# A scan over 64-token chunks: products taken from the array's two row halves in turn, and recurrent states read without block-diagonal copies

## The chip, the core and the metric

The kernel runs on one core of one Trainium2 chip, in float32 throughout. The metric is the device time of one execution in microseconds (us). The other seven cores do nothing.

## The reference, cut to what matters

One layer of a hybrid backbone over 128 context tokens and 1024 latent tokens, 1024 channels: a SwiGLU, a token mixer, a second SwiGLU, each followed by a layer norm. The change touches the recurrent branch of the mixer alone, a scan in two directions over 16 heads of 64 channels:

```python
def _rwkv7_step(S, inp):
    r, w, k, v, kk, a = inp
    sa = jnp.einsum('dbhvk,dbhk->dbhv', S, kk)
    S = S * w[..., None, :] - sa[..., :, None] * (kk * a)[..., None, :] + v[..., :, None] * k[..., None, :]
    return S, jnp.einsum('dbhvk,dbhk->dbhv', S, r)
...
s_final, y = lax.scan(_rwkv7_step, s0.astype(f32), xs)
```

Context tokens start from zero states, latent tokens from cached states. The final context states are an output.

## The kernel before, in words

The program has four stages: the first SwiGLU, the mixer's input projections and preparation, the scan, and at the end the output projections with the second SwiGLU. The change lies in the scan stage (the `with pool("s1")` block).

The 1152 tokens are cut into 18 chunks of 64 tokens, and the 16 heads into two halves of 8. So there are 36 steps. Each step treats one chunk of the forward direction (d = 0) and one of the backward direction (d = 1) for 8 heads. A tile holds two heads on its 128 partitions: the even head (e = 0) on partitions 0 to 63, the odd head (e = 1) on 64 to 127, and four such pairs i. A step consists of these pieces, all float32 on TensorE:

- `pre_lm` (line 987, tile `pa`): for each direction, pair and e, a product with a contraction over one head's 64 channels, so over one row half of the array, 128 by 128 out. VectorE multiplies it by a mask into `LM` (line 988). It is done a step or two ahead. The calls `pre_lm(s, d, 0)` and `pre_lm(s, d, 1)` are separate, with 4 products each.
- `pre_kb` (line 994, tile `pt`): transposes, copied to `KBT` by ScalarE (line 996).
- `main(s)`: line 1015 multiplies by the states. Its moving operand is `Sb`, a 128x128 tile per pair with the even head's 64x64 state in one corner and the odd head's in the other, so one product over all 128 rows serves two heads. Line 1020 adds `LM` times the values in the same accumulator `xy` (one tile of one PSUM bank per direction). ScalarE copies the sum to `Xs` (line 1024). Line 1028 multiplies by the inverse `W`, back into `xy`. ScalarE writes its negative to `vu` (line 1032). Line 1038 makes the state update `sp`. VectorE adds it to the state `Sc` (line 1039), GpSimd multiplies `Sc` by the chunk's decay (line 1040), and ScalarE copies both corners to `Sb` (lines 1041 and 1042). Line 1046 completes the outputs in `xy`, and ScalarE copies them to `yt` (line 1049).

In lines 1020, 1028 and 1046 the loop over the heads takes the two directions in turn. Their operands lie on opposite partition halves, and so do their results.

Between these pieces `fill` issues products of other work (lines 852, 854, 856: gate projections of the mixer, 128x384, in a format of one pass). They are dealt out by a table (`SPREAD`), the same number per step. A float32 product stands in the trace as two matmul records, here called passes; a transpose and a filler product are one.

Every four steps VectorE also gets one `solve`: the inversion of 32x32 triangular blocks, a chain of 31 pairs of a multiply and a subtract (lines 744 and 746) with some transposes (755 and 758). It starts from a tile `Gq`, of which one half comes by DMA into `Gt` and through ScalarE (line 739). Its result is needed some steps later.

The order of the instructions on each engine is set by a scheduler when the program is built. It runs its own timeline, so the order in the queues is not the order of the source, and each engine then takes its queue strictly as written.

Of the kernel before, what the change touches and what calls it, by code (L numbers as in the profile page):

```python
# [8 lines left out]
F32 = mybir.dt.float32  # L9
F32R = mybir.dt.float32r  # L10
AF = mybir.ActivationFunctionType
ALU = mybir.AluOpType
# [4 lines left out]
P = 128  # L17
# [43 lines left out]
def tile_step(ctx: ExitStack, tc: tile.TileContext, I: dict, O: dict):  # L61
    nc = tc.nc
    V, A, G, S, PE = nc.vector, nc.scalar, nc.gpsimd, nc.sync, nc.tensor
# [378 lines left out]
    PCst = cpool.tile([P, 2, NCHUNK, NP], F32, name="PCst")  # L442
# [10 lines left out]
    with pool("facc") as facc, pool("f1w", side="right") as wmore, pool("f1p", 6, psum=True) as psum, pool("f1a", 2, psum=True) as paux:  # L453
# [6 lines left out]
        with pool("st") as sp:  # L460
# [458 lines left out]
        for n in (6, 7):  # L919
            yield from back(*prev, n)  # L920

    with pool("s1") as pl, pool("spa", 2, psum=True) as psA, pool("spx", 2, psum=True) as psX, \
            pool("spg", 2, psum=True) as psG, pool("spm", 2, psum=True) as psM:
        maskLM = [sc[:, 0:128], sc[:, 128:256]]
        TAGP[0] = "m"
        states = {}
        for q in range(2):
            for d in range(2):
                states[q, d] = (pl.tile([P, 4, 64], F32, name=f"Sc{q}{d}"), states[0, d][1] if q else pl.tile([P, 4, P], F32, name=f"Sb{d}"))
# [4 lines left out]

        def init_ctx(hb):
            for d in range(2):
                Sc, Sb = states[0, d]
                G.memset(Sc, 0.0)
                G.memset(Sb, 0.0)
                S.dma_start(states[1, d][0], I["state"][d][:, 4 * hb:4 * hb + 4])  # L940

        def init_lat():
            for d in range(2):
                Sc, Sb = states[1, d]
                A.copy(Sb[0:64, :, 0:64], Sc[0:64])
                A.copy(Sb[64:128, :, 64:128], Sc[64:128])

        ctxs = {}

# [25 lines left out]
                c["ak"][s].append(ak)  # L975
            c["LM"][s], c["KBT"][s] = {}, {}

        def pre_lm(s, d, e):
            c = ctxs[s // 2]
            ak = c["ak"][s][d]  # L980
            if e == 0:
                c["LM"][s][d] = pl.tile([P, 4, 2, P], F32, name=f"LM{d}", tag=f"LM{d}", bufs=2)
            mk = maskLM[d].unsqueeze(1).broadcast_to([P, 4, P])
            es = slice(e * 64, e * 64 + 64)
            pa = psA.tile([P, 4, P], F32, name="pa", tag="pa")
            for i in range(4):
                PE.matmul(pa[:, i, :], ak[es, i, 128:256], ak[es, i, 0:128], start=True, stop=True)  # L987
            V.tensor_tensor(c["LM"][s][d][:, :, e, :], pa, mk, ALU.mult)

        def pre_kb(s, d):  # L990
            c = ctxs[s // 2]
# [6 lines left out]
        def main(s):  # L998
# [13 lines left out]
            for d in range(2):  # L1012
                Sb = states[q, d][1]
                for i in range(4):
                    PE.matmul(xys[d][:, 2 * i:2 * i + 2, :], ak[d][:, i, 0:128], Sb[:, i, :], start=(i == 0), stop=False, skip_group_check=True)  # L1015
            for h in range(8):
                for d in range(2):
                    x0, x1 = XR[d]
                    y0, y1 = YR[d]
                    last = PE.matmul(xys[d][x0:x1, h, :], LM[d][y0:y1, h // 2, h % 2, x0:x1], vu[d][y0:y1, h, :], start=False, stop=True, skip_group_check=True)  # L1020
            between(s, 0, last)
            for d in range(2):
                x0, x1 = XR[d]
                A.copy(Xs[x0:x1], xys[d][x0:x1])
            for h in range(8):
                for d in range(2):
                    x0, x1 = XR[d]
                    last = PE.matmul(xys[d][x0:x1, h, :], W[d][x0:x1, h // 2, h % 2, :], Xs[x0:x1, h, :], start=True, stop=True, skip_group_check=True)
            between(s, 1, last)
            for d in range(2):  # L1030
                x0, x1 = XR[d]
                A.mul(vu[d][x0:x1], xys[d][x0:x1], -1.0)
            for d in range(2):
                Sc, Sb = states[q, d]
                sp = psM.tile([P, 4, 64], F32, name="sp", tag="m")
                for h in range(8):
                    e = slice((h % 2) * 64, (h % 2) * 64 + 64)
                    PE.matmul(sp[e, h // 2, :], KBT[d][:, h // 2, e], vu[d][:, h, :], start=True, stop=True)
                V.tensor_tensor(Sc, Sc, sp, ALU.add)
                G.tensor_tensor(Sc, Sc, PCst[:, d, cs[d], 4 * hb:4 * hb + 4].unsqueeze(2).broadcast_to([P, 4, 64]), ALU.mult)  # L1040
                A.copy(Sb[0:64, :, 0:64], Sc[0:64])
                A.copy(Sb[64:128, :, 64:128], Sc[64:128])
            for h in range(8):
                for d in range(2):
                    y0, y1 = YR[d]
                    last = PE.matmul(xys[d][y0:y1, h, :], LM[d][:, h // 2, h % 2, y0:y1], vu[d][:, h, :], start=False, stop=True, skip_group_check=True)  # L1046
            for d in range(2):
                y0, y1 = YR[d]
                A.copy(yt[y0:y1, m[d]], xys[d][y0:y1])
# [59 lines left out]
        pre(1)  # L1109
        for s in range(2):  # L1110
            for d in range(2 - s):
                pre_lm(s, d, 0)
                pre_lm(s, d, 1)
                pre_kb(s, d)
        fl = filler(psG)
        sols = [(2, solve(1, psM))]
# [27 lines left out]
        with ExitStack():  # L1144
            for s in range(n):
                if s == 18:
                    init_ctx(1)
                if s % 18 == 2:
                    init_lat()
# [12 lines left out]
                if s + 2 < n:  # L1162
# [8 lines left out]
                hb, j = s // 18, s % 18  # L1171
                if j == 1:
                    for d in range(2):
                        S.dma_start(O["st"][d][:, 4 * hb:4 * hb + 4], states[0, d][0])
# [184 lines left out]
```

## Time and profile before

| | |
|---|---|
| median of 3 runs | 3506.33 us (3505.05 to 3511.2) |
| profiled execution, first to last instruction | 3503.5 us |
| scan stage in it | 1660 to 2388 us, 728 us |
| busy in the scan stage: TensorE, VectorE, ScalarE, GpSimd | 682.8, 380.5, 375.1, 261.4 us |
| share of the DMA engines in the scan stage | 0.63 |
| mean granted TensorE clock, whole span and scan stage | 0.964 and 0.96 |

The profile gives no time for the profiled execution but its span. The median of the three runs shown is 2.8 us longer than that span. A row of instructions by group reads: line, engine, operation, tiles written and read, shapes, count, then busy time in us, mean duration of one in ns, and the engine's idle time just before them with what ended it. A row of the timeline reads: start and length in us, then the same names, and how many follow each other. The length reaches to the modelled end of the last one, so the pitch of n passes is (length minus one duration) over n - 1.

### The profile page before, as it was taken

Reading aid. Unit: us, or ns where it says so; the run is one execution under the profiler, and the core shown is the slowest. Engines: PE = TensorE matmul, PEld = TensorE weight load, DVE = VectorE, ACT = ScalarE, POOL = GpSimd, SP = SyncE. Lnnn points to the kernel's source line nnn. Section 1 sums busy time; section 2 is a strip of 40 time slices with the busy share of each in tenths; the row PEclk is TensorE's granted clock in tenths of the full one; section 3 lists DMA queues with packets and bytes.
Section 4 is the critical chain, followed back from the end, with each engine's and each line's share of the span. In section 5 each row is a group of like instructions: output and inputs, shape, how many; then the busy total and the mean of one; then the engine's idle time right before and its main releaser. Section 6 shows DMA issues by size and latency. Waiting matters only on the chain. (4 is left out here: it accounts for less than half of the span.)

```text
span 3503.5 us, 61793 instructions
## 1 busy us (share of the span) xinstructions
PE 3325.9 (95%) x25166; PEld 3150.8 (90%) x25166; DVE 1962.7 (56%) x3237; ACT 1224.6 (35%) x2107; POOL 1348.6 (38%) x1077
## 2 busy tenths in 40 slices
PE   7999999999999999799999989998999999999997
PEld 7999999999988877598888888887999999999996
DVE  6888633357556788756365656534574332222466
ACT  4111111125534444532545555555345111111133
POOL 5111211136556666653322443157774111111144
PEclk9999999999999998799999989998999999999998
DMA  6443211123544545476557667665541111111133
GB/s 230 132 141 128 90 37 49 37 97 127 205 156 151 169 149 161 142 220 191 174 165 213 205 175 224 186 183 183 200 169 49 43 37 49 41 45 40 47 127 107
DMA packets 311421, 461.57 MB, mean 132 GB/s; under 512 B 115552, under 2 KB 211296, under 8 KB 309600
## 3 DMA queue, kind: packets, MB, share of 16 engines
q1 hardware_dynamic: 311136, 457.62, 41.1%
q8 instruction: 198, 3.24, 0.4%
q14 instruction: 87, 0.71, 0.1%
HBM read 325.44 MB, written 110.69 MB: 124 GB/s over the span
## 5 line engine op out<-in xcount | busy, mean ns | idle before, releaser
L127 POOL TENSOR_TENSOR wl<-wr,wh 128x1024 fp32r<-128x1024 f32 (+1 forms) x168 | 386.3, 2300 | 716.8 <-ACT wh L125 647.9
L125 ACT CAST wh<-wr 128x1024 fp32r<-128x1024 f32 (+1 forms) x321 | 321.9, 1012 | 829.8 <-PE po L135 424.0
L271 POOL TENSOR_TENSOR gl<-sg,gh 128x384 fp32r<-128x384 f32 x132 | 159.7, 1210 | 787.1 <-ACT gh L270 787.1
L134 PE MATMUL po<-gh,wh 128*128 128x384 f32 x1056 | 357.5, 339 | 8.5 <-ACT gh L270 4.2
L135 PE MATMUL pg<-h1l,wh 128*128 128x384 f32 x1056 | 356.4, 338 | 6.8 <-POOL h1l L143 6.8
L135 PE MATMUL po<-gl,wh 128*128 128x384 f32 x1056 | 357.3, 338 | 1.7 <-POOL gl L271 1.7
L136 PE MATMUL pg<-h3h,wl 128*128 128x384 f32 x1056 | 357.9, 339 | 0.0
L134 PE MATMUL pg<-h3h,wh 128*128 128x384 f32 x1056 | 357.6, 340 | 0.0
L134 PE MATMUL pg<-h1h,wh 128*128 128x384 f32 x1056 | 357.5, 339 | 0.0
L135 PE MATMUL pg<-h3l,wh 128*128 128x384 f32 x1056 | 356.8, 338 | 0.0
L136 PE MATMUL pg<-h1h,wl 128*128 128x384 f32 x1056 | 355.5, 337 | 0.0
L136 PE MATMUL po<-gh,wl 128*128 128x384 f32 x1056 | 355.5, 337 | 0.0
L127 DVE TENSOR_TENSOR wl<-wr,wh 128x1024 fp32r<-128x1024 f32 x153 | 223.2, 1463 | 214.8 <-ACT wh L125 214.7
L134 PE MATMUL pm<-h2h,wh 128*128 128x384 f32 x936 | 327.9, 350 | 8.5 <-ACT ga L810 5.1
L268 DVE TENSOR_TENSOR sg<-sg,pg 128x384 f32<-128x384 f32 x132 | 74.1, 561 | 464.9 <-PE pg L136 454.9
L135 PE MATMUL pm<-h2l,wh 128*128 128x384 f32 x936 | 328.3, 351 | 0.0
L136 PE MATMUL pm<-h2h,wl 128*128 128x384 f32 x936 | 328.3, 351 | 0.0
L288 DVE SCALAR_TENSOR_TENSOR ac<-po,modh,ac 128x384 f32<-128x384 f32 (+1 forms) x352 | 172.6, 515 | 95.4 <-PE po L136 95.4
L379 DVE SCALAR_TENSOR_TENSOR fm<-fm 128x512 f32<-128x512 f32 x224 | 183.8, 821 | 53.3 <-DMA fm<-in_w_mod 50.2
L134 PEld LDWEIGHTS po<-gh,wh 128*128 128x128 f32 x1056 | 199.2, 189 | 11.8 <-ACT gh L270 4.8
L135 PEld LDWEIGHTS pg<-h1l,wh 128*128 128x128 f32 x1056 | 200.3, 190 | 9.5 <-POOL h1l L143 8.9
L270 ACT CAST gh<-sg 128x384 fp32r<-128x384 f32 x132 | 67.5, 512 | 394.9 <-DVE sg L268 394.8
(289 smaller groups left out, 7681.3 us busy)
## 6 DMA issues: line engine op xcount, KB each, us to landing
wr<-in_ffn_in SPq DMA_DIRECT2D x120, 512.0 KB
ak<-ak SPq DMA_DIRECT2D x48, 768.0 KB
ak<-ak SPq DMA_DIRECT2D x72, 512.0 KB
wr<-in_w_mix SPq DMA_DIRECT2D x63, 512.0 KB
wr<-in_ffn_out SPq DMA_DIRECT2D x60, 512.0 KB
fm<-in_w_mod SPq DMA_DIRECT2D x112, 256.0 KB
sh<-pads SPq DMA_DIRECT2D x108, 130.0 KB
wr<-in_w_o SPq DMA_DIRECT2D x24, 512.0 KB
```

What stands on the lines that cost most here:

```text
L125: A.copy(h[:, :w], r[:, :w])
L127: e.tensor_tensor(l[:, :w], r[:, :w], h[:, :w].bitcast(F32), ALU.subtract)
L134: PE.matmul(ps, wh, xh, start=first and k == 0, stop=False)
L135: PE.matmul(ps, wh, xl, start=False, stop=False)
L136: PE.matmul(ps, wl, xh, start=False, stop=last and k == n - 1)
L268: lastv[0] = V.tensor_tensor(sg, sg, pu[:, :BN], ALU.mult)
L270: A.copy(gs[j, b][0][:, sl], sg)
L271: G.tensor_tensor(gs[j, b][1][:, sl], sg, gs[j, b][0][:, sl].bitcast(F32), ALU.subtract)
L288: lastv[0] = V.scalar_tensor_tensor(accs[b][:, n, s0:s1], po[:, s0:s1], modh[:, gate_i // 4, n, g:g + 1], accs[b][:, n, s0:s1], ALU.mult, ...
L379: V.scalar_tensor_tensor(jk, w, 1.0, silc[:, s, hf * 512:hf * 512 + 512], ALU.mult, ALU.mult, accum_out=part[:, kt, s, hf:hf + 1])
```

## The change: what it does

1. The block-diagonal copies `Sb` are gone, with the ScalarE copies that filled them and the two initial copies. The state product (now line 1010) multiplies `Sc` as it is, one head at a time: 16 products per step over 64 rows with 64 columns, in place of 8 over 128 rows with 128 columns. The heads e = 0 and e = 1 alternate.
2. `pre_lm` makes both e at once, product by product in turn, into two `pa` tiles. It is called once per step and direction, where there were two calls.
3. `xy` becomes one tile of two PSUM banks with a single buffer. A bank now holds the heads of one e for both directions; before, a bank held all heads of one direction.
4. The product with `W` (now line 1026) goes to a tile `us` of its own, one bank for both directions, from the pool that also holds `sp`, `pt` and the solve's products.
5. For d = 1, VectorE makes the copy to `Xs` (now line 1021) and the negative to `vu` (now line 1031). ScalarE keeps d = 0. The multiplication of `Sc` by the decay moves from GpSimd to VectorE (now line 1041).

```diff
@@ the scan stage
-    ... pool("spx", 2, psum=True) as psX
+    ... pool("spx", 1, psum=True) as psX
...
-        def pre_lm(s, d, e):
+        def pre_lm(s, d):
...
-            es = slice(e * 64, e * 64 + 64)
-            pa = psA.tile([P, 4, P], F32, name="pa", tag="pa")
+            pa = [psA.tile([P, 4, P], F32, name="pa", tag="pa") for e in range(2)]
             for i in range(4):
-                PE.matmul(pa[:, i, :], ak[es, i, 128:256], ak[es, i, 0:128], start=True, stop=True)
-            V.tensor_tensor(c["LM"][s][d][:, :, e, :], pa, mk, ALU.mult)
+                for e in range(2):
+                    es = slice(e * 64, e * 64 + 64)
+                    PE.matmul(pa[e][:, i, :], ak[es, i, 128:256], ak[es, i, 0:128], start=True, stop=True)
+            for e in range(2):
+                V.tensor_tensor(LM[:, :, e, :], pa[e], mk, ALU.mult)
...
-            xys = [psX.tile([P, 8, 64], F32, name="xy", tag="xy") for d in range(2)]
-            for d in range(2):
-                Sb = states[q, d][1]
-                for i in range(4):
-                    PE.matmul(xys[d][:, 2 * i:2 * i + 2, :], ak[d][:, i, 0:128], Sb[:, i, :], start=(i == 0), stop=False, skip_group_check=True)
+            xy = psX.tile([P, 2, 2, 4, 64], F32, name="xy", tag="xy")
+            eh = lambda t: t.rearrange("p (i e) v -> p e i v", e=2)
+            for i in range(4):
+                for d in range(2):
+                    for e in range(2):
+                        es = slice(e * 64, e * 64 + 64)
+                        PE.matmul(xy[:, e, d, i, :], ak[d][es, i, 0:128], states[q, d][es, i, :], start=(i == 0 and d == 0), stop=False,
+                                  skip_group_check=True)
...
-                A.copy(Xs[x0:x1], xys[d][x0:x1])
+                (V.tensor_copy if d else A.copy)(eh(Xs[x0:x1]), xy[x0:x1, :, d])
+            us = psM.tile([P, 8, 64], F32, name="us", tag="m")
...
-                    last = PE.matmul(xys[d][x0:x1, h, :], W[d][x0:x1, h // 2, h % 2, :], Xs[x0:x1, h, :], start=True, stop=True, skip_group_check=True)
+                    last = PE.matmul(us[x0:x1, h, :], W[d][x0:x1, h // 2, h % 2, :], Xs[x0:x1, h, :], start=True, stop=True, skip_group_check=True)
...
-                A.mul(vu[d][x0:x1], xys[d][x0:x1], -1.0)
+                if d:
+                    V.tensor_scalar(vu[d][x0:x1], us[x0:x1], -1.0, None, ALU.mult)
+                else:
+                    A.mul(vu[d][x0:x1], us[x0:x1], -1.0)
...
                 V.tensor_tensor(Sc, Sc, sp, ALU.add)
-                G.tensor_tensor(Sc, Sc, PCst[:, d, cs[d], 4 * hb:4 * hb + 4].unsqueeze(2).broadcast_to([P, 4, 64]), ALU.mult)
-                A.copy(Sb[0:64, :, 0:64], Sc[0:64])
-                A.copy(Sb[64:128, :, 64:128], Sc[64:128])
+                V.tensor_tensor(Sc, Sc, PCst[:, d, cs[d], 4 * hb:4 * hb + 4].unsqueeze(2).broadcast_to([P, 4, 64]), ALU.mult)
...
-            if s + 1 < n:
-                pre_lm(s + 1, 1, k)
+            if s + 1 < n and k == 0:
+                pre_lm(s + 1, 1)
...
-                    pre_lm(s + 2, 0, 0)
+                    pre_lm(s + 2, 0)
                 fill(2)
                 sol(s)
-                if s + 2 < n:
-                    pre_lm(s + 2, 0, 1)
                 fill(3)
```

The scheduler writes the queues anew, so the change moves more than the source tells. Three places matter.

TensorE, the state product and the product with `LM` in one step. The tiles `vu0` and `LM0` belong to d = 0, `vu1` and `LM1` to d = 1. Before:

```order
L1015 MATMUL xy_17666<-Sb0_14605,ak0_17254 128x128 x4
L1020 MATMUL xy_17666<-vu0_1_13546,LM0_17258 64x64 x4
L1015 MATMUL xy_17667<-Sb1_14607,ak1_17256 128x128 x4
L1020 MATMUL xy_17667<-vu1_1_13548,LM1_17411 64x64 x4
L1020 MATMUL xy_17666<-vu0_1_13546,LM0_17258 64x64
```

Now:

```order
L1010 MATMUL xy_16693<-Sc10_14606,ak0_16295 128x64 x2
L1010 MATMUL xy_16693<-Sc11_14607,ak1_16297 128x64 x2
L1016 MATMUL xy_16693<-vu0_1_13546,LM0_16299 64x64
L1016 MATMUL xy_16693<-vu1_1_13548,LM1_16446 64x64
L1016 MATMUL xy_16693<-vu0_1_13546,LM0_16299 64x64
```

Before, the two directions had accumulators of their own, and the queue took four products of one direction and then four of the other before it took them in turn. Now the accumulator is one tile, all state products stand ahead of all products with `LM`, and these alternate by direction from the first on.

TensorE, the products of `pre_lm`. Each `pa` tile belongs to one e, so to one row half. Now, at two steps:

```order
L979 MATMUL pa_16559<-ak0_16554 128x128
L979 MATMUL pa_16560<-ak0_16554 128x128
L979 MATMUL pa_16559<-ak0_16554 128x128
```

```order
L979 MATMUL pa_16837<-ak0_16832 128x128 x3
L1026 MATMUL us_16748<-Xs_16692,W_16046 64x64
L979 MATMUL pa_16837<-ak0_16832 128x128
L1026 MATMUL us_16748<-Xs_16692,W_16046 64x64 x15
L852 MATMUL pb_16589<-u2_14777,wh_16463 128x384
```

In the first the row halves alternate as the source has them. In the second the queue takes all four products of one half, and those of the other half (`pa_16838`) only after the products with `W` and fillers. Of the 576 products, 279 stand beside one of the other half and 297 do not.

VectorE, in a step in which a solve runs. Now:

```order
L744 TENSOR_TENSOR pr<-Wd,Gq 128x23x9
L1021 COPY Xs<-xy 64x2x4x64
L746 TENSOR_TENSOR Wd<-Wd,pr 128x23x9
L981 TENSOR_TENSOR LM_15940<-pa,sc 128x4x128
L744 TENSOR_TENSOR pr<-Wd,Gq 128x24x8
```

```order
L744 TENSOR_TENSOR pr<-Wd,Gq 128x30x2
L1031 TENSOR_SCALAR vu_0_13547<-us 64x512
L746 TENSOR_TENSOR Wd<-Wd,pr 128x30x2
```

The copy to `Xs` and the negative to `vu`, for which TensorE waits in mid-step, now stand between instructions of the solve, here 14 of them from the one to the other. From one step's first state addition to the next step's, the queue before held at most 31 instructions of a solve; now the fullest interval of each of the seven solves in the loop holds 37, 39, 38, 29, 28, 35 and 42 (before: 30, 29, 29, 31, 29, 27 and 26).

After the scan the TensorE queue is the same as before.

More of the change, by code (lines that the diff above doesn't have):

```diff
@@ L920, in filler @@
             yield from back(*prev, n)
-    with pool("s1") as pl, pool("spa", 2, psum=True) as psA, pool("spx", 2, psum=True) as psX, \
+    with pool("s1") as pl, pool("spa", 2, psum=True) as psA, pool("spx", 1, psum=True) as psX, \
             pool("spg", 2, psum=True) as psG, pool("spm", 2, psum=True) as psM:
@@ L928, in tile_step @@
             for d in range(2):
-                states[q, d] = (pl.tile([P, 4, 64], F32, name=f"Sc{q}{d}"), states[0, d][1] if q else pl.tile([P, 4, P], F32, name=f"Sb{d}"))
+                states[q, d] = pl.tile([P, 4, 64], F32, name=f"Sc{q}{d}")
         base = [(0, (0, 1)), (0, (1, 0))] + [(1, (2 + i, 17 - i)) for i in range(16)]
@@ L936, in init_ctx @@
             for d in range(2):
[L937 to L942, printed above, removed]
-            for d in range(2):
-                Sc, Sb = states[1, d]
-                A.copy(Sb[0:64, :, 0:64], Sc[0:64])
-                A.copy(Sb[64:128, :, 64:128], Sc[64:128])
+                G.memset(states[0, d], 0.0)
+                S.dma_start(states[1, d], I["state"][d][:, 4 * hb:4 * hb + 4])
         ctxs = {}
@@ L976, in pre @@
             c["LM"][s], c["KBT"][s] = {}, {}
-        def pre_lm(s, d, e):
+        def pre_lm(s, d):
             c = ctxs[s // 2]
             ak = c["ak"][s][d]
-            if e == 0:
-                c["LM"][s][d] = pl.tile([P, 4, 2, P], F32, name=f"LM{d}", tag=f"LM{d}", bufs=2)
+            LM = c["LM"][s][d] = pl.tile([P, 4, 2, P], F32, name=f"LM{d}", tag=f"LM{d}", bufs=2)
             mk = maskLM[d].unsqueeze(1).broadcast_to([P, 4, P])
-            es = slice(e * 64, e * 64 + 64)
-            pa = psA.tile([P, 4, P], F32, name="pa", tag="pa")
+            pa = [psA.tile([P, 4, P], F32, name="pa", tag="pa") for e in range(2)]
             for i in range(4):
-                PE.matmul(pa[:, i, :], ak[es, i, 128:256], ak[es, i, 0:128], start=True, stop=True)
-            V.tensor_tensor(c["LM"][s][d][:, :, e, :], pa, mk, ALU.mult)
+                for e in range(2):
[3 more added lines that the diff above has]
+                V.tensor_tensor(LM[:, :, e, :], pa[e], mk, ALU.mult)
         def pre_kb(s, d):
@@ L1010, in main @@
             yt = c["yt"]
-            xys = [psX.tile([P, 8, 64], F32, name="xy", tag="xy") for d in range(2)]
-            for d in range(2):
-                Sb = states[q, d][1]
-                for i in range(4):
-                    PE.matmul(xys[d][:, 2 * i:2 * i + 2, :], ak[d][:, i, 0:128], Sb[:, i, :], start=(i == 0), stop=False, skip_group_check=True)
+            xy = psX.tile([P, 2, 2, 4, 64], F32, name="xy", tag="xy")
[6 more added lines that the diff above has]
+                                  skip_group_check=True)
             for h in range(8):
@@ L1019, in main @@
                     y0, y1 = YR[d]
-                    last = PE.matmul(xys[d][x0:x1, h, :], LM[d][y0:y1, h // 2, h % 2, x0:x1], vu[d][y0:y1, h, :], start=False, stop=True, skip_group_check=True)
+                    last = PE.matmul(xy[x0:x1, h % 2, d, h // 2, :], LM[d][y0:y1, h // 2, h % 2, x0:x1], vu[d][y0:y1, h, :], start=False, stop=True,
+                                     skip_group_check=True)
             between(s, 0, last)
@@ L1045, in main @@
                     y0, y1 = YR[d]
-                    last = PE.matmul(xys[d][y0:y1, h, :], LM[d][:, h // 2, h % 2, y0:y1], vu[d][:, h, :], start=False, stop=True, skip_group_check=True)
+                    last = PE.matmul(xy[y0:y1, h % 2, d, h // 2, :], LM[d][:, h // 2, h % 2, y0:y1], vu[d][:, h, :], start=False, stop=True,
+                                     skip_group_check=True)
             for d in range(2):
                 y0, y1 = YR[d]
-                A.copy(yt[y0:y1, m[d]], xys[d][y0:y1])
+                A.copy(eh(yt[y0:y1, m[d]]), xy[y0:y1, :, d])
                 if s % 2 == 1 and other(cs[d] // 2, d) <= s % 18:
@@ L1111, in tile_step @@
             for d in range(2 - s):
-                pre_lm(s, d, 0)
-                pre_lm(s, d, 1)
+                pre_lm(s, d)
                 pre_kb(s, d)
@@ L1147, in tile_step @@
                     init_ctx(1)
-                if s % 18 == 2:
-                    init_lat()
                 after[0] = main(s)
@@ L1173, in tile_step @@
                     for d in range(2):
-                        S.dma_start(O["st"][d][:, 4 * hb:4 * hb + 4], states[0, d][0])
+                        S.dma_start(O["st"][d][:, 4 * hb:4 * hb + 4], states[0, d])
                 for tt in range(9):
```

4 lines of the change are left out of this document (1 added, 3 removed).

## The prediction

> **What bounds the kernel now.** I read the stretches first, to see how full TensorE is in the scan stage, then its groups there, then single stretches of its timeline for the price of a pass, then the waits, then VectorE.
>
> ```profile
> 1660.00:2388.00 728.00, 682.82 (x9619) 611.29 (x9616) 380.53 (x771) 375.08 (x699) 261.39 (x230) 0.96 0.63 187
> ```
>
> The columns are stretch, length, busy time of TensorE, its weight loads, VectorE, ScalarE and GpSimd, then granted clock, DMA share and GB/s. TensorE is busy 683 of 728 us; the other 45 it waits. So TensorE work taken away is time, unless a wait takes its place. Who ends these waits:
>
> ```profile
> PE sp L1038 <- ACT vu L1032: 15.4, 7, 5.7
> PE pt L994 <- DVE Sc L1039: 14.4, 7, 3.0
> PE pa L987 <- DVE LM L988: 6.1, 5, 3.6
> PE xy L1028 <- ACT Xs L1024: 4.0, 1, 4.0
> ```
>
> VectorE ends 20.5 us of them, ScalarE 19.4. On average VectorE is half idle (380 of 728), but not where a solve runs:
>
> ```profile
> 2229.58 0.41 DVE L1039 TENSOR_TENSOR Sc<-Sc,sp 128x256 f32<-128x256 f32 x1
> 2244.70 0.41 DVE L1039 TENSOR_TENSOR Sc<-Sc,sp 128x256 f32<-128x256 f32 x1
> ...
> 2232.00:2242.00 10.00, 10.00 (x123) 8.99 (x121) 9.55 (x22) 5.38 (x11) 1.28 (x1) 1.00 0.47 151
> ```
>
> From one state addition to the next step's, 15.1 us pass here, and within them VectorE is busy 9.55 of 10 us and TensorE 10 of 10. In such a step both are full: lighten one and load the other, and the other sets the pace.
>
> **The price of a pass on TensorE.**
>
> ```profile
> 24.43 1.84 PE L481 MATMUL pmod<-cc,w 128*128 128x2 f32 x16
> 2101.02 1.02 PE L1020 MATMUL xy<-vu,LM 64*64 64x64 f32 x14
> 2105.38 1.71 PE L987 MATMUL pa<-ak 64*128 64x128 f32 x16
> 2116.74 1.50 PE L1015 MATMUL xy<-Sb,ak 128*128 128x128 f32 x12
> 2118.18 1.15 PE L1020 MATMUL xy<-vu,LM 64*64 64x64 f32 x32
> 2123.12 1.16 PE L987 MATMUL pa<-ak 64*128 64x128 f32 x8
> 2124.21 0.44 PE L854 MATMUL pb<-u,wh 128*128 128x384 f32 x1
> ```
>
> ```profile
> L987 PE MATMUL pa<-ak 64*128 64x128 f32 x1145 | 151.2, 290 | 6.1 <-DVE LM L988 6.1
> L1015 PE MATMUL xy<-Sb,ak 128*128 128x128 f32 x576 | 79.7, 282 | 0.1
> L1046 PE MATMUL xy<-vu,LM 128*64 128x64 f32 x1152 | 57.3, 238 | 0.0
> L1020 PE MATMUL xy<-vu,LM 64*64 64x64 f32 x1152 | 56.1, 223 | 0.0
> L1028 PE MATMUL xy<-Xs,W 64*64 64x64 f32 x1152 | 52.2, 226 | 4.0 <-ACT Xs L1024 4.0
> ```
>
> Pitch is (length minus one duration) by (count minus one). The state products: (1.50 - 0.28) / 11 = 0.111 us. Line 481 has weights just as wide but only 2 columns: (1.84 - 0.25) / 15 = 0.106, no cheaper. So with 128-wide weights a pass costs 0.11 us, however few its columns. Line 1020 with one direction alone: (1.02 - 0.22) / 13 = 0.061. With both in turn: (1.15 - 0.22) / 31 = 0.030. Opposite halves run side by side. Last, changing the array's shape: the 8 passes from 2123.12 to the next start at 2124.21 take 1.09 us, 0.19 more than 8 x 0.112. That is what a stretch of another shape costs.
>
> **The change part by part, TensorE.** Counts are from the queues, prices from the rows above.
>
> *State products.* Before, 16 passes per step at 0.112. Now 32, as 16 side-by-side pairs with 128-wide weights, at 0.112 a pair. Gain 0. The bounds: if 64 columns brought the price of 0.061, it is 16 x 0.05 x 36 = 29 us less; if the halves don't overlap, 16 x 0.112 x 36 = 64 us more. Line 481 decides for the middle.
>
> *`pre_lm`.* A product is two passes, 0.224 us alone, 0.112 as one of a pair. The queue lets 279 of the 576 alternate: -31 us. The other 297 gain nothing, since the scheduler put one half's four products ahead of the other's. But the old queue already had some 37 places where one half's four directly follow the other's, and there the array overlapped them: the 16 passes at 2105.38 took 1.71, where 16 x 0.112 and one entry and tail (0.1 + 0.18) make 2.07. That is 37 x 0.36 = 13 us already had. Net -18.
>
> *Products with `LM` and `W`.* Today's groups are busy 56.1 + 52.2 = 108 us. Wholly in turn they would take 36 x 1.15 x 2 = 83, or 86 at the stage's clock of 0.96. The old queue takes all 16 in turn in only 14 steps (`LM`) and 11 (`W`), the new one in 33 and 30. So about -21.
>
> *Outputs (line 1046, now 1045).* Some 110 products stood in one-direction stretches, and now next to none; each saves one of its two passes of 0.06: -6.
>
> *Shapes.* Outside the products with `LM` and `W`, whose stretches are in their busy time, the queue's stretches of one shape go from 409 to 414: +1.
>
> Sum on TensorE: 0 - 18 - 21 - 6 + 1 = **-44 us**.
>
> **VectorE.** It gets four instructions a step.
>
> ```profile
> L744 DVE TENSOR_TENSOR pr<-Wd,Gq 128x31 f32<-128x31 f32 (+15 forms) x221 | 107.4, 486 | 64.8 <-ACT vu L1032 21.8 <-PE sp L1038 20.5 <-DMA Wd<-in_id 16.4
> L988 DVE TENSOR_TENSOR LM<-pa,sc 128x512 f32<-128x512 f32 x144 | 96.4, 684 | 113.1 <-PE pa L987 103.9 <-PE xy L1046 8.7
> L746 DVE TENSOR_TENSOR Wd<-Wd,pr 128x135 f32<-128x135 f32 (+15 forms) x222 | 95.5, 430 | 5.7
> L1039 DVE TENSOR_TENSOR Sc<-Sc,sp 128x256 f32<-128x256 f32 x72 | 29.9, 417 | 70.7 <-PE sp L1038 68.2 <-ACT wh L125 2.0
> ...
> L1032 ACT ACTIVATE vu<-xy 64x512 f32<-64x512 f32 x72 | 42.6, 592 | 40.2 <-PE xy L1028 39.2
> L1024 ACT COPY Xs<-xy 64x512 f32<-64x512 f32 x72 | 41.8, 581 | 57.2 <-PE xy L1020 56.4
> L1041 ACT COPY Sb<-Sc 64x256 f32<-64x256 f32 x71 | 28.7, 405 | 61.6 <-POOL Sc L1040 60.7
> L1042 ACT COPY Sb<-Sc 64x256 f32<-64x256 f32 x71 | 28.6, 402 | 1.4
> ...
> L1040 POOL TENSOR_TENSOR Sc<-Sc,PCst 128x256 f32<-128x256 f32 x71 | 45.3, 649 | 121.3 <-DVE Sc L1039 119.1 <-PE pt L994 2.2
> ```
>
> None of the four stands on VectorE in the trace. For `Xs` and `vu` the nearest rows are ScalarE's 0.58 and 0.59, and VectorE's 0.68 for a tile of the same width from PSUM; I take 0.6 (0.55 to 0.7). For the decay the nearest is the addition of the same size, 0.42; GpSimd's 0.65 is the upper end. Together 2 x 0.6 + 2 x 0.42 = 2.0 us a step, 73 us in all. In the steps without a solve VectorE's idle half covers it.
>
> In the fullest step of a solve nothing does. An instruction of a solve is (107.4 + 95.5) / 443 = 0.46 us. Before, that step holds about 29 of them: 13.3 us, with two additions (0.8), three masks (2.0) and a gate product (0.5) 16.7 us, about TensorE's own. Now it holds 28 to 42, on average 35: 16.1 + 3.3 + 2.0 = 21.4 us. TensorE's step falls by 44 / 36 = 1.2 to about 15.5. And TensorE can't run ahead, since `Xs` and `vu` stand in mid-queue and their time within the step is fixed too. So it waits about 6 us in this step and some 1.5 in the fuller neighbour: 7.5 x 7 solves = 53 us, where VectorE ends 20.5 today: **+33**. The bounds: 20.5 again (0 more), if VectorE does the queue's solve work in the idle time of the neighbouring steps; 75 (+55), if each point at which TensorE waits in the step adds its own lateness.
>
> *The solve's start.* VectorE also stands still until `Gq` is there:
>
> ```profile
> 1811.63 1.92 ACT L739 COPY Gq<-Gt 64x1024 f32<-64x1024 f32 x1 [4.42 <-DMA Gt<-qd]
> 1814.22 1.12 PE L1038 MATMUL sp<-vu,KBT 128*64 128x64 f32 x16 [5.74 <-ACT vu L1032]
> 1814.90 0.19 DVE L744 TENSOR_TENSOR pr<-Wd,Gq 128x31 f32<-128x31 f32 x1 [17.50 <-ACT vu L1032]
> ```
>
> ScalarE waits 4.42 us for the DMA with `vu` queued behind it, and TensorE 5.74 for `vu`. The first solve instruction waits for the same copy, now with `Xs` and `vu` of d = 1 queued behind it: +5 (0 to 10).
>
> *ScalarE* loses four copies of 0.40, one of 0.58 and one of 0.59, 2.8 us of its 10.4 a step, and makes halves of `Xs` and `vu` beside VectorE: of 19.4 us of waits for it, -4 (0 to -12); what follows `Gq` stays. *GpSimd* loses 45 us that nobody waits for. *The single `xy`*: the next step's first state product waits for both copies to `yt`, 2 x 0.58, while TensorE has two groups of transposes and up to twelve fillers to do; nothing, or 0.6 x 36 = 21 us if that cover is gone.
>
> Sum: -44 + 33 + 5 - 4 = **-10**. Against the profiled execution 3503.5 - 10 = 3493.5; the median of the runs is 2.8 above its span, so 3496.
>
> **The rivals.**
>
> *The whole gain stays.* VectorE works the solves off elsewhere, and its waits stay at 20.5: -44 - 4 = -48, so 3458; half of that, 3475, if it partly does. For it: VectorE has 350 idle us in the stage. Against: its queue is fixed, and the instructions stand in these steps.
>
> *VectorE's queue costs more than TensorE saves.* The place is the wait for `Xs` and `vu` in the full step; its price is the upper bound, +55, with +5 for `Gq`: -44 + 60 = +16, so 3522. It decides from 65 us of waits for VectorE on. For it: both engines full in the rows above, and two new waits in mid-step. Against: ScalarE's half is free.
>
> *Sharing a bank.* `LM` and `W` products of the two directions, on opposite row halves, now write the same bank. If that made them take turns, 32 passes go from 0.03 to 0.06 each, twice a step: 36 x 2 x 0.95 = 68 us, so 3564.
>
> ```profile
> 2121.00 0.19 PE L768 MATMUL ph<-DT,Nt 32*32 32x32 f32 x1
> 2121.01 0.19 PE L768 MATMUL ph<-Dx,Nt 32*32 32x32 f32 x1
> ```
>
> Against it: these two sit on opposite rows, write different partitions of one `ph` tile, so one bank, and start 10 ns apart. The Trainium skill says otherwise: on the page "TensorEngine Tiling (Array Packing)", section "Restrictions and Gotchas", different row tiles cannot access the same PSUM bank at once. By that rule the time is this rival's; the pair above does not bear it out where the partitions differ.
>
> *64 columns halve the state product's pass*: 29 us less, 3467; line 481 speaks against it.
>
> **How the numbers follow.** Forecast 0.45 (own range 3482 to 3512), whole or half gain 0.22, VectorE costs more 0.25, shared bank 0.04, cheap state pass 0.04. The range is from 3460 to 3526, both first rivals in. Changes below 0.2% (7 us) can't be told from none. Faster: 0.25 of the forecast's share, 0.22 and 0.04, 0.51; same: 0.18 and 0.05, 0.23; slower: 0.02, 0.20 and 0.04, 0.26.
>
> **What would show it.** Groups: the state product's 1152 passes busy near 80 us again; `LM` and `W` near 42 each; `pre_lm` some 20 below 151. Waits: TensorE for VectorE's `Xs` and `vu`, together with `Sc` and `LM`, near 53. Stretches: VectorE 9.5 of 10 with TensorE below 8 in the seven solves. Waits for VectorE near 20 would make it wrong downwards; 65, or pitches of 0.06 in `LM` and `W`, upwards.

## The result, and the profile after

The changed kernel takes 3636.36 us (median) against 3505.69 us for the kernel before beside it: ratio 1.0374, 95% interval 1.0351 to 1.0398. It is 131 us slower; I had forecast 10 us faster, and a range that ended at 3526. One of its four runs took 5008.51 us, at a clock of 0.586 over the whole run; it is in the median, but not in the ratio.

All of it is in the scan stage. Up to 1660 us TensorE is busy 1568 us in both kernels, and after the scan stage the last stage takes 1115 us as before (3636.6 - 2521, 3503.5 - 2388). So the stage runs from 1660 to 2521, 861 us in place of 728. The stretch row of the changed kernel (columns as in the prediction):

```profile
1660.00:2521.00 861.00, 689.63 (x10088) 610.64 (x10089) 444.14 (x901) 270.41 (x472) 213.20 (x155) 0.87 0.53 158
```

TensorE is busy 690 us, 7 more than before, at a clock of 0.87 where it was 0.96. It is idle 172 us, where it was 45. The lower clock hides how much work was saved, so a third figure is used below: TensorE's busy time in each stretch of 2 us, times the clock of that stretch, summed over the stage. It estimates what the work would have taken at full clock. It is 653 us before and 609 now; the rest of the busy time, 30 and 81 us, is what the lower clock cost. So the 133 us are 127 of idle time and 51 of lost clock, less 44 of work saved. (In five runs with the old products the estimate lies between 649 and 668, so it is good to some 10 us.)

TensorE's waits in the stage (total, times, longest):

```profile
PE us L1026 <- ACT Xs L1021: 72.9, 14, 15.1
PE us L1026 <- DVE Xs L1021: 44.1, 20, 5.8
PE sp L1039 <- DVE vu L1031: 27.8, 9, 5.8
PE pt L987 <- DVE Sc L1040: 10.8, 8, 4.0
PE pa L979 <- DVE LM L981: 8.5, 6, 3.5
```

VectorE ends 91 us, where I had 53; but the largest row is ScalarE's `Xs`, 72.9 where it was 4.0, and I had expected ScalarE's share to shrink. What waits for `Xs` is the product with `W`:

```profile
L1026 PE MATMUL us<-Xs,W 64*64 64x64 f32 x1152 | 65.2, 266 | 118.4 <-ACT Xs L1021 72.9 <-DVE Xs L1021 44.1 <-ACT yo L1100 1.4
```

Of the four groups that I had put prices on, the state product (83.6 us busy, forecast 80) and `LM` (44.9, forecast 42) came near, `pre_lm` (146.2, forecast 131) and `W` (65.2, forecast 42) did not. A pass of `W` takes 266 ns on average where it took 226: much of this group runs right behind a wait, at the lower clock shown below.

At full clock the prices of TensorE's passes are as forecast. One step of the timeline of the changed kernel:

```profile
2431.57 1.11 PE L1010 MATMUL xy<-Sc,ak 64*128 64x64 f32 x16
2434.23 1.15 PE L1016 MATMUL xy<-vu,LM 64*64 64x64 f32 x32
```

(1.11 - 0.28) / 15 = 0.055 per pass of the state product, 0.11 a pair. The products with `LM` run at (1.15 - 0.23) / 31 = 0.030 with both directions in one bank, just as they did in two. The Trainium skill ("TensorEngine Tiling (Array Packing)", "Restrictions and Gotchas") says that different row tiles cannot access one PSUM bank at the same time. These 0.030 us do not bear that out where the two write different partitions.

One place shows what went wrong. ScalarE at the start of a solve, first the kernel before, then the changed one:

```profile
1802.98 0.58 ACT L1024 COPY Xs<-xy 64x512 f32<-64x512 f32 x1
1805.40 0.59 ACT L779 ACTIVATE Wb<-ph 32x512 f32<-32x512 f32 x1 [1.85 <-PE ph L768]
1806.00 0.59 ACT L780 ACTIVATE Wb<-ph 32x512 f32<-32x512 f32 x1
1806.62 0.59 ACT L996 COPY KBT<-pt 128x512 f32<-128x512 f32 x1
1811.63 1.92 ACT L739 COPY Gq<-Gt 64x1024 f32<-64x1024 f32 x1 [4.42 <-DMA Gt<-qd]
1813.57 1.21 ACT L1032 ACTIVATE vu<-xy 64x512 f32<-64x512 f32 x2
```

```profile
1822.84 1.92 ACT L739 COPY Gq<-Gt 64x1024 f32<-64x1024 f32 x1 [14.12 <-DMA Gt<-qd]
1824.78 0.59 ACT L779 ACTIVATE Wb<-ph 32x512 f32<-32x512 f32 x1
1825.38 0.59 ACT L780 ACTIVATE Wb<-ph 32x512 f32<-32x512 f32 x1
1825.99 0.59 ACT L989 COPY KBT<-pt 128x512 f32<-128x512 f32 x1
1826.47 0.58 ACT L1021 COPY Xs<-xy 64x512 f32<-64x512 f32 x1
```

`Gq` stood behind `Xs`; now it stands ahead of it, and so do the three instructions that follow it. ScalarE waits 14.12 us for the DMA, with the `Xs` that TensorE needs queued behind. (This is the longest of the seven such waits; the others are 0.9 to 8 us.) TensorE, same kernel, same place:

```profile
1827.11 0.47 PE L1026 MATMUL us<-Xs,W 64*64 64x64 f32 x2 [11.45 <-ACT Xs L1021]
1832.69 1.97 PE L1026 MATMUL us<-Xs,W 64*64 64x64 f32 x30 [5.11 <-DVE Xs L1021]
```

The second wait is for VectorE's `Xs`, which stands behind 21 instructions of the solve; the first of them started as soon as `Gq` was there. And then the clock, in four stretches of the changed kernel around the two waits (columns as above; the clock is third from the end):

```profile
1804.00:1816.00 12.00, 11.66 (x239) 10.14 (x237) 1.84 (x3) 2.28 (x5) 1.26 (x1) 1.00 0.75 226
1816.00:1827.00 11.00, 0.00 (x0) 0.00 (x0) 1.94 (x9) 4.11 (x5) 0.00 (x0) 0.64 0.46 136
1827.00:1837.00 10.00, 4.78 (x43) 4.23 (x45) 9.29 (x24) 0.64 (x2) 0.00 (x0) 0.55 0.51 149
1837.00:1847.00 10.00, 6.87 (x106) 6.27 (x103) 9.53 (x23) 3.23 (x6) 0.36 (x1) 1.00 0.01 2
```

After 11 us without work the next 10 us run at a clock of 0.55. So this wait is paid twice, as idle time and as slow work behind it.

### The profile page after: what moved, and what is told of

It reads as the page before. It is cut to its first block, busy times and chain, and to the rows that moved or that the text cites. A ratio compares the mean times of both kernels' runs of the same rounds, so it can differ in the third digit from the quotient of the medians.

```text
span 3636.6 us, 62709 instructions
## 1 busy us (share of the span) xinstructions
PE 3336.8 (92%) x25742; PEld 3154.7 (87%) x25742; DVE 2030.0 (56%) x3381; ACT 1121.3 (31%) x1883; POOL 1299.5 (36%) x1001
## 5 line engine op out<-in xcount | busy, mean ns | idle before, releaser
L135 PEld LDWEIGHTS po<-gl,wh 128*128 128x128 f32 x1056 | 200.5, 190 | 4.1 <-POOL gl L271 4.1
```

Of the source, the lines that this page charges most:

```text
L135: PE.matmul(ps, wh, xl, start=False, stop=False)
```

## The experiments

Each ratio is to the kernel before on the same chip, with a 95% interval. The expectations name four theories. A: VectorE's halves of `Xs` and `vu` wait in series behind ScalarE's. B: VectorE is overfull where a solve runs. C: late work of several kinds stands in the helpers' queues (ScalarE, VectorE, GpSimd) ahead of what TensorE waits for. D: it is the solve's places alone.

### VectorE's part taken out (theory A: series, theory B: VectorE overfull)

In the changed kernel VectorE's halves of `Xs` and `vu` wait for ScalarE's halves, which read the same bank:

```profile
DVE Xs L1021 <- ACT Xs L1021: 60.8, 14, 10.7
DVE vu L1031 <- ACT vu L1033: 46.5, 19, 4.6
```

My prediction had them side by side. So the first four runs took VectorE's new instructions out, together and apart, and put them alone into the kernel before.

```diff
-                (V.tensor_copy if d else A.copy)(eh(Xs[x0:x1]), xy[x0:x1, :, d])
+                A.copy(eh(Xs[x0:x1]), xy[x0:x1, :, d])
...
-                if d:
-                    V.tensor_scalar(vu[d][x0:x1], us[x0:x1], -1.0, None, ALU.mult)
-                else:
-                    A.mul(vu[d][x0:x1], us[x0:x1], -1.0)
+                A.mul(vu[d][x0:x1], us[x0:x1], -1.0)
```

> The changed kernel, but Xs and vu of d = 1 are made on ScalarE again; the decay stays on VectorE and all TensorE products stay as changed. Theory A (VectorE's half waits in series behind ScalarE's half, since both read one bank): TensorE's 72 us of waits for VectorE's Xs and vu vanish, and most of the 73 us for ScalarE's Xs too, because ScalarE's queue is no longer held up by what waits for VectorE; the time is 3470 to 3500. Theory B (my prediction's: VectorE is overfull in the solve steps): the same 72 us vanish and the clock recovers a part, but ScalarE's own lateness stays, 3500 to 3540. Theory C (ScalarE's queue now has late work in front of Xs, whoever makes the other half): the 73 us for ScalarE's Xs stay or grow, 3560 to 3600.

Measured: 3633.43 us, 1.036 (1.032 to 1.040). TensorE's waits for VectorE's `Xs` and `vu` are gone, but those for the state rose from 10.8 us to

```profile
PE pt L987 <- DVE Sc L1037: 50.0, 11, 8.9
```

What was taken off one wait came back at another.

```diff
-                V.tensor_tensor(Sc, Sc, PCst[:, d, cs[d], ...
+                G.tensor_tensor(Sc, Sc, PCst[:, d, cs[d], ...
```

> The changed kernel, but the decay multiplication is on GpSimd again; VectorE keeps its halves of Xs and vu. Theory A: the decay is not the cause, 3610 to 3650. Theory B: 31 us of VectorE's work leave the overfull steps, a fifth of the extra waits goes with them, 3590 to 3615. Theory C: 3620 to 3650.

Measured: 3640.39 us, 1.0378 (1.0341 to 1.0415). With both edits:

> The TensorE part of the change alone: Xs and vu on ScalarE for both directions, decay on GpSimd, all products, tiles and the missing block-diagonal copies as changed. My prediction's terms give TensorE -44 and ScalarE -4 and nothing for VectorE: 3458. Theories A and B: 3455 to 3480. Theory C: 3540 or more, since ScalarE's queue is as disturbed without VectorE's halves. If the shared bank made the LM and W products take turns, 3520 or more and pitches near 0.06 in them.

Measured: 3617.52 us, 1.0314 (1.0267 to 1.0360). And the kernel before with those instructions on VectorE alone:

```diff
-                A.copy(Xs[x0:x1], xys[d][x0:x1])
+                (V.tensor_copy if d else A.copy)(Xs[x0:x1], xys[d][x0:x1])
...
-                G.tensor_tensor(Sc, Sc, PCst[:, d, cs[d], ...
+                V.tensor_tensor(Sc, Sc, PCst[:, d, cs[d], ...
```

(`vu` likewise.)

> The kernel before, with only the four VectorE instructions moved: Xs and vu of d = 1 and both decays on VectorE, Sb copies and all products as before. Here each direction has its own bank, and VectorE's copy waits for TensorE, not for ScalarE. Theory A: no series, so about no change, 3495 to 3525. Theory B: VectorE is as overfull as in the changed kernel but TensorE is slower by 44, so waits grow by some 30, 3520 to 3560. Theory C: 3510 to 3530.

Measured: 3548.04 us, 1.0117 (1.0073 to 1.0162). Theories A and B fall as the cause: without any work moved to VectorE, 112 of the 131 us are still there. VectorE's part costs 42 us by itself (its queues were written anew as well, which is in the 42), near the 34 that my terms for VectorE, the solve's start and ScalarE add up to. But of the waits that I had put behind that term hardly any are in this run, where TensorE waits for VectorE's `vu` and `Xs` so long:

```profile
PE sp L1041 <- DVE vu L1033: 2.6, 2, 2.4
PE xy L1028 <- DVE Xs L1024: 2.3, 2, 1.8
```

The TensorE part alone, stage and waits:

```profile
1660.00:2502.00 842.00, 686.25 (x10119) 607.88 (x10120) 363.31 (x759) 313.96 (x544) 256.77 (x225) 0.86 0.54 162
```

```profile
PE us L1026 <- ACT Xs L1021: 58.6, 14, 10.6
PE pt L987 <- DVE Sc L1037: 53.3, 13, 7.2
PE pa L979 <- DVE LM L981: 19.2, 8, 3.9
```

### The solve's places (theory D)

In the queue of this kernel the 62 VectorE instructions of a solve stand for instance as 47 and 15, 35 and 27 or 31 and 31 ahead of successive state additions; in the kernel before as 12, 30 and 20 or 9, 31 and 22. So I put the solve back: `Gq` behind `Xs`, the chain in three pieces, by an order of issue without a wait.

```diff
+            begin(s, 0, xs0)
...
+            begin(s, 1, add)
+            begin(s, 2, add)
...
+        def begin(s, j, ins):
+            if begun and s == begun[0][0] + j // 2:
+                with tc.issue_after(ins.ins):
+                    next(begun[0][1])
```

> The TensorE part alone (as in the run before that had Xs, vu on ScalarE and the decay on GpSimd), but the solve is pinned to the places that it had in the kernel before: ScalarE's Gq copy behind the step's Xs, and the 62 VectorE instructions as 12, 28 and 22 around three successive state additions (in the run without the pins they stand as 24 to 47 and the rest, in two). Theory D (the new queues put Gq ahead of Xs and bunch the solve's chain, so every solve step stalls): the solve steps fall from 30 to 44 us back to about 25, 8 x 12 = 96 us less, 3500 to 3530, and if all of the pace returns, with TensorE's saving, 3460 to 3480. Theory C (ScalarE's queue is disturbed in general, by the group norm's and the fillers' work as well): 3570 to 3600.

Measured: 3598.14 us, 1.0258 (1.0224 to 1.0291).

> The whole change with the solve pinned in the same way (Gq behind ScalarE's Xs; 12, 28 and 22 VectorE instructions around three successive state additions). Theory D: 3480 to 3530. My prediction's working has this spread of the solve as its lower bound for VectorE's waits: 3460 to 3480. Theory C: 3590 to 3620.

Measured: 3635.01 us, 1.0369 (1.0329 to 1.0409), no gain that can be told. The reverse, in the kernel before (the solve's loads are also issued a little earlier in the program there, so that `Xs` can be put behind `Gq`):

```diff
+                    if s == 3 or s > 3 and s % 4 == 2 and s < 28:
+                        es.enter_context(tc.issue_after(gq[0].ins))
                     A.copy(Xs[x0:x1], xys[d][x0:x1])
```

> The kernel before with one thing forced: in the step in which a solve starts, ScalarE's Gq copy, which waits for a DMA, stands ahead of Xs in its queue and not behind it, as in the changed kernel. All arithmetic is as before. Theory D: each of 7 solves loses 5 to 10 us, 3540 to 3590. Theory C: 3505 to 3530.

Measured: 3541.92 us, 1.0108 (1.0069 to 1.0147). So `Gq` ahead of `Xs` costs at most some 38 us; more than that one item moved, for two of the seven solves stand there as 34 and 28, and as 25, 27 and 10. Putting the solve back gains 19 in the TensorE part and nothing in the whole change. Theory D is a part at most. With the solve back, other late work stands in front. ScalarE in the TensorE part with the solve put back, then VectorE:

```profile
2365.29 0.63 ACT L1091 ACTIVATE y<-y 128x512 f32<-128x512 f32 x1 [9.77 <-POOL y L1090]
...
2374.76 0.51 ACT L1217 CAST gh<-gh 128x384 fp32r<-128x384 f32 x1 [6.01 <-DMA gh<-gd_d]
2375.17 1.18 ACT L1026 COPY Xs<-xy 64x512 f32<-64x512 f32 x2
```

```profile
2243.48 1.23 DVE L759 STREAM_TRANSPOSE DT<-Wb 32x1024 f32<-32x1024 f32 x1 [8.15 <-DMA Wb<-ed]
2245.28 2.53 DVE L762 STREAM_TRANSPOSE Wb<-Dx 32x1024 f32<-32x1024 f32 x2 [0.57 <-DMA Dx<-ed]
2247.84 0.75 DVE L1043 TENSOR_TENSOR Sc<-Sc,sp 128x256 f32<-128x256 f32 x2
```

A square of the group norm waits 9.77 us for GpSimd and a cast of the next stage 6.01 for a DMA, both ahead of `Xs`; two transposes of the solve wait for DMAs ahead of the state additions. This is what theory C says: not one item, but late work of several kinds.

### Which edit moves the queues

> The kernel before with only the pre_lm products of both halves in turn, in two pa tiles; states, Sb, xy and all else as before. The solve keeps its places in the queues here. My prediction's term: -18, so 3488. Theory D: 3480 to 3500, since the order stays. Theory C has no forecast of its own; a time above 3530 would put the loss into this part.

Measured: 3502.22 us, 0.9993 (0.9973 to 1.0013). The solve stands nearly where it stood, no loss, but no 18 us of gain either. (The edit is that of `pre_lm` and its calls in the diff of the change, by itself.) Its stage:

```profile
1660.00:2382.00 722.00, 665.28 (x9475) 592.72 (x9475) 374.37 (x758) 369.63 (x686) 255.62 (x225) 0.93 0.62 186
```

The work did shrink, by some 33 us at full clock (620), but idle time rose by 12 us and the lost clock by 15, so the profiled stage is 6 us shorter.

> The kernel before with only the state product changed: 16 half-row products with Sc as it is, Sb and its copies gone, xy as one tile of two banks; pre_lm, the W product into xy, Xs, vu and the decay as before. My prediction priced this at 0 on TensorE and -4 on ScalarE: 3500. Theory C: the solve's places in the queues are the disturbed ones here too (Gq ahead of Xs, 62 VectorE instructions in two steps), so 3570 to 3620.

Measured: 3627.76 us, 1.0371 (1.0338 to 1.0404). This kernel does not compute the layer: part of the output sums is lost, probably because the `W` product starts a new accumulation in a bank that now holds both directions. The instructions and their sizes are those of the edit. The state product with its tile `xy` moves the queues (the solve stands for instance as 36 and 26 or 43 and 19 there), and with them comes the whole loss.

### The order held

The three helpers' queues of the stage, written out in the order that the scheduler gave them in the kernel before; all arithmetic, tiles and TensorE products as in the TensorE part alone. TensorE's and SP's queues are left to the scheduler, so their order moves along.

```diff
+    for e, runs in ORDER.items():
+        mine = [i for i in nc.cur_bb.bb.instructions[T0:] if i.engine == e and ...]
+        row = [mine[k] for a, n in runs for k in range(a, a + n)]
+        for p, i in zip(row, row[1:]):
+            tc.add_manual_dep(i, p.name, ...NoSync..., reason="order")
```

> The TensorE part alone (states as they are, products in turn, xy and us as changed; Xs, vu on ScalarE, decay on GpSimd), with the queues of ScalarE, VectorE and GpSimd in the scan stage written out in the very order that the scheduler gave them in the kernel before (the Sb copies left out). TensorE's and SP's queues are the scheduler's. Theory C (the new queues of the helpers put late work, fed by DMA or GpSimd, ahead of what TensorE waits for): the loss is gone and TensorE's saving shows, 3465 to 3500. A theory that puts the loss into the products or tiles themselves (one xy, us in the pool of sp and pt): 3570 to 3620, as without the pins.

Measured: 3516.15 us, 1.0046 (1.0027 to 1.0065): 101 us less than with the scheduler's own order.

> The same, with SP's queue, which issues the loads, also in the order of the kernel before. Theory C: within 10 us of the run with three queues pinned, unless loads are issued too late there; then up to 20 less. The other theory: 3570 to 3620.

Measured: 3534.94 us, 1.0116 (1.0074 to 1.0159). Holding SP's queue too did not help; why it takes some 19 us more I did not find out. The reverse, the disturbed order under the old products:

> The kernel before, all arithmetic and tiles as before, with the queues of ScalarE, VectorE and GpSimd in the scan stage in the order that they have in the run of the TensorE part alone (3617). If the order is the cause: 3590 to 3640. If it only goes along with it: 3505 to 3540.

Measured: 3658.58 us, 1.0443 (1.0419 to 1.0468), slower than the changed kernel itself. The stretch and two waits, first of the run with the old order under the new products, then of the new order under the old products:

```profile
1660.00:2398.00 738.00, 669.49 (x10089) 596.23 (x10088) 378.09 (x764) 311.85 (x539) 254.40 (x224) 0.91 0.62 184
```

```profile
PE pa L1034 <- DVE LM L1036: 25.0, 11, 6.2
PE us L1081 <- ACT Xs L1076: 3.9, 2, 3.4
```

```profile
1660.00:2547.00 887.00, 766.10 (x9493) 679.36 (x9492) 362.09 (x758) 370.28 (x691) 256.39 (x227) 0.85 0.51 152
```

```profile
PE pt L1039 <- DVE Sc L1084: 52.1, 12, 11.9
PE xy L1073 <- ACT Xs L1069: 44.8, 11, 7.0
```

The long waits for `Xs` and `Sc` go with the order, not with the products, and so does most of the lost clock. With the old products TensorE's busy time is 766 us at a clock of 0.85, 83 more than before for the same work (657 us at full clock, 653 before). The two runs together show the cause of the loss: the order of the helpers' queues. Two things they don't separate: TensorE's and SP's queues, which moved with them, and what an order costs just because it was written for other products.

### Where the saving goes

With the old order back, TensorE's saving should have shown: 3458 by my terms. It is 3516, above the kernel before. To test the premise itself I left out work that nothing waits for: the middle product of each three fillers (line 854; the text of the first of the two runs says 852, which is the product before it).

```diff
             PE.matmul(ps, wh, xh, start=k == 0, stop=False)
             yield
-            PE.matmul(ps, wh, xl, start=False, stop=False)
             yield
```

> The kernel before, with the queues of ScalarE, VectorE and GpSimd in the scan stage kept in their order, and a third of the fillers left out (the middle product of each three at line 852, so the gate projections lose their low-order term): 299 passes of 0.214 us start to start, 64 us of TensorE work that nothing waits for, spread evenly. My prediction's premise (TensorE is busy 683 of 728 us, so work taken away is time): 3440 to 3450. The other view (the round trips through the helpers set the pace, and freed time comes back as idle time and as half clock after it): 3480 to 3505.

Measured: 3522.10 us, 1.0069 (1.0045 to 1.0092), slower with less work. TensorE's own queue had moved there too, so again with all five queues held:

> The kernel before, all five queues of the scan stage held in their order, with the middle product of each three fillers (line 854) left out, so the gate projections lose a low-order term: 300 passes of 0.229 us start to start, 69 us of TensorE work that nothing waits for. My prediction's premise (TensorE is the bound, work taken away is time): 3435 to 3450. The other view (round trips through the helpers set the pace; freed time comes back as idle time, and as half clock behind it): 3480 to 3525.

Measured: 3490.26 us, 0.9963 (0.9942 to 0.9985).

```profile
1660.00:2371.00 711.00, 647.98 (x9178) 572.60 (x9177) 377.93 (x758) 367.83 (x686) 255.60 (x225) 0.91 0.63 188
```

Of 69 us taken away, 17 come through in the profiled stage and 14 in the medians. By the same three figures: the work fell by 65 us (588 at full clock, where 69 were taken away), idle time rose by 18 (711 - 648 = 63), and the lost clock by 30 (60). -65 + 18 + 30 = -17. In this trace the queues of TensorE and the helpers stand as in the kernel before, the fillers aside. So TensorE, though busy 683 of 728 us, isn't the bound by itself: part of the freed time becomes idle time, and the larger part is lost to the clock. That the round trips through the helpers set the pace fits this, but no run singles one out.

The same sum for the TensorE part with the old order: the work fell by 44 (609), just what I had added up, idle time rose by 23 and the lost clock by 30 (60), and the stage is 10 us longer.

### What is left

> States multiplied as they are, xy in two banks, W product to us; pre_lm as before (no pairs), Xs, vu and decay as before, and ScalarE's, VectorE's and GpSimd's queues in the order of the kernel before. If the order was the whole loss and pairs in held places cost the last 12 us: 3495 to 3506. If us in the pool of sp and pt costs something by itself: 3510 to 3530.

Measured: 3528.78 us, 1.0086 (1.0057 to 1.0115), so the pairs are not what costs the last 12 us; without them it is no less. It lies where I had put a cost of `us` in the pool of `sp` and `pt`, but this run doesn't single that out either.

> As the run with the three queues in the old order (all TensorE changes, pairs included, 3516), but the LM masks on VectorE are left to the scheduler. If the 25 us of waits of pre_lm for the masks there are what is left of the loss: 3490 to 3505. If the freed TensorE time comes back anyway: 3505 to 3525.

Measured: 3536.92 us, 1.0096 (1.0077 to 1.0116), above both expectations; waits for the masks grew from 25.0 to 43.7 us.

If late work ahead of `vu` is what the kernel before pays for, moving that one item should help it:

> The kernel before, the helpers' queues of the scan stage in their order, with one item moved: in the seven solve steps ScalarE's Gq copy, which waited 19.6 us for its DMA in all with vu behind it, stands behind both vu instead. If the place of DMA-fed work is what counts: TensorE's 15.4 us of waits for vu shrink, and some half clock behind them, 3490 to 3500. If the later start of the solve's chain gives it back: 3500 to 3515.

Measured: 3524.14 us, 1.0066 (1.0038 to 1.0094), above both expectations. The profiled execution is the shortest of the eight (3504.1 us). In it the waits for `vu` did fall:

```profile
PE sp L1099 <- ACT vu L1093: 4.7, 3, 2.3
```

from 15.4, and `Gq`'s own from 19.6 to 3.4. But TensorE's queue was not held, and it is busy 698 us there at the same clock, 15 more. So this run does not tell what the place of `Gq` is worth; as a kernel it is no better.

> The TensorE part of the change with the helpers' queues in the old order (3516) and Gq behind both vu. If that one item holds TensorE's saving back: 3480 to 3500. If freed time comes back at other waits (masks, Sc): 3505 to 3520.

Measured: 3533.03 us, 1.0086 (1.0053 to 1.0118), above both again. No version that was run and computes everything beats the kernel before by more than can be told.

## Why the prediction was wrong, step by step

**TensorE's sum, -44: right as work, wrong as time.** The pair of state passes (0.11), the pitch with `LM` (0.030) and no cost for the shared bank came as forecast; the work came out at -44 at full clock, in the changed kernel and with the old order, give or take 10. The step that failed stands at the top of the prediction: "TensorE work taken away is time, unless a wait takes its place". Of 69 us of fillers 17 came through; of the 18 us for pairs in `pre_lm`, none that can be told from zero. The reading behind it, 683 of 728 us busy, took work at half clock for load: at full clock that work is 653 us.

**The queues: the term that was missing, and the largest.** I compared the queues at three places and used them to count VectorE's instructions in a step. I did not ask, queue by queue, which instructions wait for a DMA or GpSimd, and whether they now stand ahead of `Xs`, `vu`, `Sc` or `LM`. The queues were known, and ScalarE's shows it, before:

```
L1024 COPY Xs<-xy 64x512 x2
L779 ACTIVATE Wb_13538<-ph 32x16x32
L780 ACTIVATE Wb_13538<-ph 32x16x32
L996 COPY KBT_16393<-pt 128x512
L739 COPY Gq<-Gt 64x1024
L1032 ACTIVATE vu_1_13546<-xy 64x512
```

and now:

```
L739 COPY Gq<-Gt 64x1024
L779 ACTIVATE Wb_13538<-ph 32x16x32
L780 ACTIVATE Wb_13538<-ph 32x16x32
L989 COPY KBT_16409<-pt 128x512
L1021 COPY Xs<-xy 64x2x4x64
L1033 ACTIVATE vu_1_13546<-us 64x512
```

For ScalarE the prediction had -4 and "what follows `Gq` stays"; this was therefore the step that failed here, with "+5 (0 to 10)" for the solve's start. Measured, the new order costs 101 us under the new products and 154 under the old.

**The clock: not costed.** I took the stage's 0.96 for the new kernel. It was 0.87, and what the clock cost within the busy time went from 30 to 81 us.

**VectorE's queue, +33: near in size, not in kind.** Its instructions alone cost 42 us in the kernel before. But TensorE's waits for VectorE's `Xs` and `vu` were 4.9 us there, not 33, and in the changed kernel, where they were 72, taking VectorE's halves away gained nothing that can be told (3633 against 3636). That the halves run in series, not side by side, was missed as well, and it is not the cause either.

**The single `xy`, 0: right.** The state product waits for nothing in the changed kernel's groups:

```profile
L1010 PE MATMUL xy<-Sc,ak 64*128 64x64 f32 x1136 | 83.6, 276 | 0.0
```

**Rivals.** "VectorE's queue costs more than TensorE saves" had the right sign, 16 us in place of 131, and the wrong place. None of the four was late work in the helpers' queues. Two slips in the sums change nothing here: the +16 leaves out ScalarE's -4, and the range starts at 3460, though the rival that it is said to hold stands at 3458.

Open: why the state product moves the scheduler's order (only that it does was seen); what holds the pace once the order is back; what `us` in the pool of `sp` and `pt` costs; the 19 us of SP's queue; what part TensorE's own order has. The whole change with all helpers in the old order was not run, nor the kernel before with all five queues held and its fillers kept.

## What to carry to other kernels

Where a scheduler writes the queues, compare them engine by engine ahead of any sum: look for instructions fed by a DMA or a slow helper, and for what the full engine waits for behind them. Hold the old order under the new work, and the new order under the old work: two runs tell an order's cost from the edit's, if TensorE's queue is held too. And test that an engine is the bound by leaving out work that nothing waits for; a busy share that is partly half clock proves nothing.

## What the runs showed of the hardware

The stage's clock was 0.96 before, 0.93 with the pairs alone, and 0.91 both with the new products under the old order and, all queues held, with a third of the fillers left out. Each of these takes work from TensorE, and in each the lower clock ate a good part of the saving. It also fell without less work, to 0.85 with the new order under the old products, where TensorE was idle 121 us. The Trainium skill ("TensorE: Matmul & The Clock Gate", "What's actually happening") has the half clock as the default state, released after a busy window of about 3.4 us. The trace agrees: in stretches of 1 us around the long wait above, TensorE works until 1815.7, and again without a break from 1832.7 on. The clock:

```profile
1818.00:1819.00 1.00, 0.00 (x0) 0.00 (x0) 0.00 (x0) 0.00 (x0) 0.00 (x0) 1.00 0.56 184
1819.00:1820.00 1.00, 0.00 (x0) 0.00 (x0) 0.00 (x0) 0.00 (x0) 0.00 (x0) 0.51 0.37 116
1835.00:1836.00 1.00, 1.00 (x4) 1.00 (x4) 1.00 (x2) 0.28 (x1) 0.00 (x0) 0.50 0.00 0
1836.00:1837.00 1.00, 1.00 (x8) 0.75 (x9) 0.93 (x4) 0.00 (x0) 0.00 (x0) 0.95 0.00 0
```

It drops to half some 3.4 us after the last product and is back some 3.4 us after TensorE works steadily again. The 0.47 us of work at 1827.11 did not bring it back. This is one place, read to about 0.1 us.
